# Second feed-forward products of a transformer block: residual rows loaded a tile a step, sums and stores of results spread over later steps, fewer buffers for the inputs of block two

## The chip, the cores and the metric

The kernel runs on one core of a Trainium2 chip. The metric is the device time of one execution in microseconds; the time of a kernel is the median of its runs. Beside the timed runs one execution was profiled. It has a time of its own, and all lines of the profile belong to that execution.

The engines in the profile: PE does matmuls (PEld loads their weights), DVE is the vector engine, ACT the scalar engine, POOL the third engine for elementwise work, and SP issues nearly all DMAs of this kernel. Each engine takes its instructions in the order of its own queue and waits at an instruction until what it needs is there.

## What is computed

One layer of a diffusion backbone over 2048 latent tokens of width 1024, with 256 context tokens: attention and a gated MLP side by side, their merge, and a feed-forward layer. All is float32. The change lies in the feed-forward layer:

```python
def sq_relu_mlp(h, w1, w2):
    return jnp.square(jax.nn.relu(h @ w1)) @ w2
...
        h2 = modulate(x, norm2_g[l], sh2, sc2)
        x = x + g2 * sq_relu_mlp(h2, w_ff1[l], w_ff2[l])
```

`x` is (2048, 1024), `w1` is (1024, 4096), `w2` is (4096, 1024). The residual `x`, which is added last, is the result of the merge; the kernel keeps it in DRAM (`x1_d`, shown as `x_d` in the profile).

## The kernel before

**Precision.** Each float32 operand is split into a high part (fp32r, the cast of L1291 on ACT) and a remainder (the subtraction of L1292 on DVE). A product is three matmuls: high by high, high by low, low by high (`product`, L1195 to L1197).

**Two blocks, seven products.** The tokens are worked in two blocks of 1024. In each block `ff1` makes the activations and `ff2` multiplies them by `w2`, both with Strassen's scheme in Winograd's form: the 2 x 2 grid of quarter matrices takes seven products of sums and differences instead of eight. `ff1` (L1256) writes its seven activation operands to DRAM (`ao_d`); the seven operands of `w2` are written once, in block one (`w2o_d` in the profile). `ff2` (L1296) reads both back.

**The steps of `ff2`.** The products come in the order 0, 1, 5, 6, 4, 2, 3. Each has 8 chunks (`NCH`) of its inner dimension, so there are 56 steps of one chunk. A step multiplies 4 tiles (`TT`) of 128 tokens by 512 columns, each in a PSUM bank of its own: 2 x 3 matmuls a tile. `ff2_chunk` (L1285) loads a chunk: for the activations and for the weights, one 512 KB load on SP, a cast on ACT, a subtraction on DVE. It is called two steps ahead; its four tiles have the tag f4, of which there are 12.

**What leaves.** After the last chunk of a product, `take` (L1327) empties the bank of each tile. Product 0 is copied to u2 (L1331) and stays in the bank; product 1 is added in the same bank and gives the first quarter of the result, whereupon u2 is copied back into the bank (L1334) and products 5 and 6 go on from there, each copied out as u2 and u3. Products 4 and 2 are added to u3 and u2 on DVE; product 3 goes on in the bank that product 6 left. A finished quarter goes through `leave` (L1318): a multiplication by the gate `g2b`, an addition of the residual tile `xs[t]`, and a store to `out`. All these additions and multiplications are recorded under L1304, the helper `tt`: f<-b,g2b is the multiplication from PSUM (products 1 and 3), f<-f,g2b that of products 4 and 2, f<-f,b the sum with u3 or u2, f<-f,f the residual's addition. `residual` (L1309) loads all four tiles of residual rows, 256 KB each, in the step of the last chunk. The stores (L1325) are put off by one step: they are issued after the chunk loads of the next step.

**The inputs of block two.** While `ff2` of block one runs, one piece of `h_ops` (L1004) is done after each step: in four passes of five pieces it fetches rows of `x1_d` (L985, four DMAs in pieces of 512 bytes, f8 tiles), scales them on DVE (L992), transposes them on PE (L182), reads the four transposed tiles out on ACT (L999), makes four sums and differences on DVE (L1019 to L1028) and splits seven tiles into halves (L970 on ACT, L971 on DVE).

**The f2 tiles.** u2, u3, xs, c, the transposed tiles of `h_ops` and its s1 to s4 all have the tag f2: 128 x 512 floats, 16 of them in all (L58).

**What sets the order.** The program names instructions in an order, but a planner puts each engine's queue together at build time by when it reckons operands to be ready. `order` (L1442) adds constraints to it: a tile of a tag begins after the tile of that tag named before it, and on SP the instructions named within `ff2` keep the program's order (`self.loads`). DVE's, ACT's and PE's order within `ff2` is the planner's.

Of the kernel before, what the change touches and what calls it, by code (L numbers as in the profile page):

```python
# [18 lines left out]
P = 128  # L19
# [10 lines left out]
TB = 512  # L30
NB = SEQ // TB
TT = TB // P
# [11 lines left out]
NCH = NG // 2  # L44
# [23 lines left out]
class Kern:  # L68
# [935 lines left out]
    def h_ops(self, blk, ops):  # L1004
        nc = self.nc
        add, sub = ALU.add, ALU.subtract
        at = self.here()
        rb = self.h_rstd(blk)
        self.pins.append(range(at, self.here()))
        for kk in range(KC // 2):  # L1010
            x = self.h_fetch(blk, kk)
            self.h_scaled(x, rb)
            yield
            raw = {(i, j): self.h_turn(x, kk, i, j) for j in range(2) for i in range(2)}
            yield
            s1, s2, s3, s4 = (self.sb("f2", [TB]) for _ in range(4))
            tt = nc.vector.tensor_tensor
            ops[0][kk] = self.halves(kk, 0, raw[0, 0])
            tt(out=s1, in0=raw[1, 0], in1=raw[1, 1], op=add)  # L1019
            tt(out=s2, in0=s1, in1=raw[0, 0], op=sub)  # L1020
            ops[5][kk] = self.halves(kk, 5, s2)
            yield
            ops[1][kk] = self.halves(kk, 1, raw[0, 1])
            tt(out=s3, in0=raw[0, 0], in1=raw[1, 0], op=sub)
            ops[6][kk] = self.halves(kk, 6, s3)
            yield
            ops[4][kk] = self.halves(kk, 4, s1)
            tt(out=s4, in0=raw[0, 1], in1=s2, op=sub)  # L1028
            ops[3][kk] = self.halves(kk, 3, raw[1, 1])
            ops[2][kk] = self.halves(kk, 2, s4)  # L1030
            yield

    def h_early(self):
# [262 lines left out]
    def ff2(self, blk, side):  # L1296
        nc = self.nc
        add, mult = ALU.add, ALU.mult
        ready = self.ready + [self.ff2_chunk(blk, 0, 1)]
        begin = self.here()  # L1300
        late = []

        def tt(out, in0, in1, op):
            nc.vector.tensor_tensor(out=out, in0=in0, in1=in1, op=op)  # L1304

        goes = {1: (0, 0), 4: (1, 1), 2: (0, 1), 3: (1, 0)}
        u2, u3, xs = ([None] * TT for _ in range(3))

        def residual(p):  # L1309
            i, j = goes[p]  # L1310
            for t in range(TT):
                xs[t] = self.sb("f2", [TB])
                nc.sync.dma_start(
                    xs[t],
                    self.x1_d[2 * blk + i][t * P : (t + 1) * P, j * TB : (j + 1) * TB],
                )

        def leave(p, t, src):  # L1318
            i, j = goes[p]
            row = (2 * blk + i) * TB + t * P  # L1320
            cs = slice(j * TB, (j + 1) * TB)
            c = self.sb("f2", [TB])
            tt(c, src, self.g2b[:, cs], mult)
            tt(c, c, xs[t], add)
            late.append(lambda: nc.sync.dma_start(self.out[0, row : row + P, cs], c))  # L1325

        def take(p, t):  # L1327
            ps = banks[p][t]
            if p == 0:
                u2[t] = self.sb("f2", [TB])  # L1330
                nc.scalar.copy(u2[t], ps)  # L1331
            elif p == 1:
                leave(p, t, ps)
                nc.scalar.copy(ps, u2[t])  # L1334
            elif p in (5, 6):
                u = u2 if p == 5 else u3
                u[t] = self.sb("f2", [TB])
                nc.scalar.copy(u[t], ps)
            elif p in (4, 2):
                u = u3[t] if p == 4 else u2[t]  # L1340
                tt(u, u, ps, add)
                leave(p, t, u)
            else:
                leave(p, t, ps)

        order = (0, 1, 5, 6, 4, 2, 3)
        steps = [(p, c) for p in order for c in range(NCH)]
        banks = {}
        for n, (p, c) in enumerate(steps):
            if n + 2 < len(steps):  # L1350
                ready.append(self.ff2_chunk(blk, *steps[n + 2]))
            for f in late:
                f()
            late.clear()
            (ah, al), (wh, wl) = ready.pop(0)
            fresh = p in (0, 4)
            if c == 0 and fresh:
                new = [self.bank([TB]) for _ in range(TT)]
                for other in (0, 1, 5, 6, 3) if p == 0 else (4, 2):
                    banks[other] = new  # L1360
            if c == NCH - 1 and p in goes:
                residual(p)
            for t in range(TT):
                tok = slice(t * P, (t + 1) * P)
                a = [(ah[:, s, tok], al[:, s, tok]) for s in range(2)]
                b = [(wh[:, s], wl[:, s]) for s in range(2)]
                self.product(banks[p][t], a, b, fresh and c == 0)
                if c == NCH - 1:
                    take(p, t)
            next(side, None)  # L1370
        for f in late:
            f()
        for _ in side:
            pass
        self.loads.append(range(begin, self.here()))
# [329 lines left out]
```

## Time and profile before

| what | us |
|---|---|
| median of 3 runs | 3104.24 |
| lowest and highest of them | 3098.3 and 3105.01 |
| the profiled execution | 3103.83 |
| its span, first to last instruction | 3102.0 |
| mean granted TensorE clock | 0.994 |

On the span's scale `ff2` of block one runs from about 2150 to 2475 us, `ff1` of block two from there to about 2780, and `ff2` of block two from there to the end at 3102. The timeline's rows give the start, the duration, the engine, the line, the operation, the tiles written and read, the shapes, a count where rows were merged, and in brackets the idle time of the engine before it with what ended it. SPq and DVEq are the queues' own instructions. A row of waits gives total us, number and longest. A row by windows gives, for each stretch, the busy time and count of PE, PEld, DVE, ACT and POOL, then the granted clock, the share of DMA and GB/s.

### The profile page before, as it was taken

Reading aid. Unit: us, or ns where it says so; the run is one execution under the profiler, and the core shown is the slowest. Engines: PE = TensorE matmul, PEld = TensorE weight load, DVE = VectorE, ACT = ScalarE, POOL = GpSimd, SP = SyncE. Lnnn points to the kernel's source line nnn. Section 1 sums busy time; section 2 is a strip of 40 time slices with the busy share of each in tenths; the row PEclk is TensorE's granted clock in tenths of the full one; section 3 lists DMA queues with packets and bytes.
Section 4 is the critical chain, followed back from the end, with each engine's and each line's share of the span. In section 5 each row is a group of like instructions: output and inputs, shape, how many; then the busy total and the mean of one; then the engine's idle time right before and its main releaser. Section 6 shows DMA issues by size and latency. Waiting matters only on the chain.

```text
span 3102.0 us, 37971 instructions
## 1 busy us (share of the span) xinstructions
PE 3042.7 (98%) x13892; PEld 2299.5 (74%) x13892; DVE 1972.1 (64%) x2893; ACT 1356.6 (44%) x2058; POOL 704.1 (23%) x539
## 2 busy tenths in 40 slices
PE   8999999999999999999999999999999999999999
PEld 4888888887555555555877878887777888888777
DVE  5837576576776767667643488876654676654545
ACT  4443435342555554544322255444543344444433
POOL 0000000010888888886144300000000000000000
PEclk9999999999999999999999999999999999999999
DMA  6354756544000000003754548887575644445565
GB/s 218 111 175 120 226 156 192 165 142 132 26 14 15 15 4 18 11 8 118 253 180 156 164 148 320 315 306 256 201 246 210 210 150 155 157 147 192 204 216 204
DMA packets 332173, 485.42 MB, mean 156 GB/s; under 512 B 33969, under 2 KB 166321, under 8 KB 331986
## 3 DMA queue, kind: packets, MB, share of 16 engines
q1 hardware_dynamic: 324002, 478.38, 46.3%
q10 hardware_dynamic: 7984, 4.61, 0.5%
q8 instruction: 109, 1.79, 0.2%
q14 instruction: 78, 0.64, 0.1%
HBM read 348.56 MB, written 134.35 MB: 156 GB/s over the span
## 4 chain that ended last, share of the span: by engine, by line
PE 89%; DMA 5%; DVE 3%; ACT 1%; issue 1%; POOL 1%; SPq 0%; DVEq 0%; ACTq 0%; POOLq 0%
PE b L1196 12%; PE b L1197 12%; PE b L1195 11%; PE b L176 10%; PE b L178 10%; PE b L177 10%; PE b L1597 8%; PE b L1564 5%; PE b L1583 4%; PE b L1529 3%; PE b L182 2%; DMA f<-w2o_d 1%; DMA bw<-in_w_br_gm 1%; POOL bw L148 1%; DMA f<-x_d 1%
## 5 line engine op out<-in xcount | busy, mean ns | idle before, releaser
L1292 DVE TENSOR_TENSOR f<-f,f 128x1024 fp32r<-128x1024 f32 x224 | 273.2, 1224 | 274.6 <-ACT f L1291 271.0
L1540 DVE TENSOR_REDUCE ts<-b 128x1 f32<-128x512 f32 x512 | 314.6, 681 | 173.2 <-PE b L1529 173.2
L1291 ACT CAST f<-f 128x1024 fp32r<-128x1024 f32 x224 | 235.2, 1053 | 335.3 <-DMA f<-ao_d 288.9
L1196 PE MATMUL b<-f,f 128*128 128x512 f32 x896 | 351.3, 392 | 4.6 <-DVE f L1292 4.0
L1197 PE MATMUL b<-f,f 128*128 128x512 f32 x896 | 349.6, 390 | 0.0
L1195 PE MATMUL b<-f,f 128*128 128x512 f32 x896 | 307.4, 392 | 10.3 <-ACT b L1334 4.7
L1613 POOL TENSOR_TENSOR ac<-ac,p 128x512 f32<-128x512 f32 x216 | 296.6, 1406 | 71.1 <-ACT p L1587 70.4
L1587 ACT ACTIVATE p<-b 128x512 f32<-128x512 f32 x384 | 199.4, 615 | 159.3 <-PE b L1583 142.5
L1613 POOL TENSOR_TENSOR ac<-ac,t 128x512 f32<-128x512 f32 x160 | 231.9, 1476 | 1.4 <-ACT t L1587 1.4
L1196 PE MATMUL b<-hl,f 128*128 128x512 f32 x576 | 224.9, 391 | 1.6 <-DVE hl L971 1.5
L1195 PE MATMUL b<-hl,f 128*128 128x512 f32 x576 | 224.1, 389 | 0.0
L1197 PE MATMUL b<-hl,f 128*128 128x512 f32 x576 | 224.0, 389 | 0.0
L148 DVE TENSOR_TENSOR w<-w,w 128x1024 fp32r<-128x1024 f32 x120 | 146.6, 1222 | 99.1 <-ACT w L144 70.6
L1195 PEld LDWEIGHTS b<-f,f 128*128 128x128 f32 x896 | 168.1, 188 | 51.0 <-ACT f L1291 6.8
L176 PE MATMUL b<-t,w 128*128 128x512 f32 x512 | 202.8, 396 | 0.1
L1196 PEld LDWEIGHTS b<-f,f 128*128 128x128 f32 x896 | 168.8, 188 | 45.7 <-DVE f L1292 11.2
L1564 PE MATMUL b<-t,t 128*128 128x512 f32 x576 | 198.4, 415 | 1.7 <-ACT p L1587 1.6
L178 PE MATMUL b<-t,w 128*128 128x512 f32 x512 | 199.7, 390 | 0.0
L177 PE MATMUL b<-t,w 128*128 128x512 f32 x512 | 199.5, 390 | 0.0
L1197 PEld LDWEIGHTS b<-f,f 128*128 128x128 f32 x896 | 168.5, 188 | 34.6
L176 PE MATMUL b<-w,t 128*128 128x512 f32 (+1 forms) x528 | 191.0, 362 | 1.0 <-ACT t L440 1.0
L144 ACT CAST w<-w 128x1024 fp32r<-128x1024 f32 x120 | 126.1, 1050 | 150.0 <-DMA w<-in_w_in 118.3
(226 smaller groups left out, 6289.6 us busy)
## 6 DMA issues: line engine op xcount, KB each, us to landing
w<-in_w_in SPq DMA_DIRECT2D x120, 512.0 KB
ao_d<-f SPq DMA_DIRECT2D x224, 256.0 KB
f<-ao_d SPq DMA_DIRECT2D x112, 512.0 KB
f<-w2o_d SPq DMA_DIRECT2D x112, 512.0 KB
f<-in_w_ff SPq DMA_DIRECT2D x48, 1024.0 KB
w2o_d<-f SPq DMA_DIRECT2D x112, 256.0 KB
md<-in_w_mod SPq DMA_DIRECT2D x32, 512.0 KB
f<-x_d SPq DMA_DIRECT2D x64, 256.0 KB
```

The source lines that it names most:

```text
L176: mm(ps, sh, mh, start=start, stop=False)
L177: mm(ps, sh, ml, start=False, stop=False)
L178: mm(ps, sl, mh, start=False, stop=stop)
L1195: mm(ps, wh, hh, start=start and k == 0, stop=False, skip_group_check=True)
L1196: mm(ps, wh, hl, start=False, stop=False, skip_group_check=True)
L1197: mm(ps, wl, hh, start=False, stop=k == len(w) - 1, skip_group_check=True)
L1291: nc.scalar.copy(h, f32(l))
L1292: nc.vector.tensor_tensor(out=l, in0=f32(l), in1=f32(h), op=ALU.subtract)
L1540: nc.vector.tensor_reduce(out=self.mx[:, t, h, c : c + 1], in_=ps[h], axis=AX.X, op=ALU.max)
L1564: self.nc.tensor.matmul(self.pts[j][h], k.KA[c][self.kv][:, ks], self.qa[h], start=True, stop=False, skip_group_check=True,)
L1597: nc.tensor.matmul(self.o[h * HD : (h + 1) * HD, :], k.V[c][:, i, self.kv * HD : (self.kv + 1) * HD], pt[h], start=j == 0, stop=j == NKT - 1,)
L1613: nc.gpsimd.tensor_tensor(out=self.acc[e][:, h], in0=old[:, h], in1=pt[h], op=ALU.add)
```

## The change

In `h_ops`, the differences are written over transposed tiles that are no longer needed, so that a pass takes five f2 tiles instead of eight; the difference for product 6 is made one piece earlier. In `ff2`, `residual` loads one tile, and is called in each of the last four steps of a product that leaves, with the tile's number. `leave` only multiplies; the addition of the residual and the store are put on the list `late` together. From that list one entry is taken before tile 0 and one before tile 2 of a step, except in a product's last step, so that the four entries go in two steps. After the last product they are all worked off behind the loop, as the stores were before.

```diff
--- before.py
+++ after.py
@@ -1013,21 +1013,22 @@
             yield
             raw = {(i, j): self.h_turn(x, kk, i, j) for j in range(2) for i in range(2)}
             yield
-            s1, s2, s3, s4 = (self.sb("f2", [TB]) for _ in range(4))
             tt = nc.vector.tensor_tensor
-            ops[0][kk] = self.halves(kk, 0, raw[0, 0])
-            tt(out=s1, in0=raw[1, 0], in1=raw[1, 1], op=add)
-            tt(out=s2, in0=s1, in1=raw[0, 0], op=sub)
-            ops[5][kk] = self.halves(kk, 5, s2)
+            r00, r01, r10, r11 = (raw[i, j] for i in range(2) for j in range(2))
+            s1 = self.sb("f2", [TB])
+            ops[0][kk] = self.halves(kk, 0, r00)
+            tt(out=s1, in0=r10, in1=r11, op=add)
+            tt(out=r10, in0=r00, in1=r10, op=sub)
+            tt(out=r00, in0=s1, in1=r00, op=sub)
+            ops[5][kk] = self.halves(kk, 5, r00)
             yield
-            ops[1][kk] = self.halves(kk, 1, raw[0, 1])
-            tt(out=s3, in0=raw[0, 0], in1=raw[1, 0], op=sub)
-            ops[6][kk] = self.halves(kk, 6, s3)
+            ops[1][kk] = self.halves(kk, 1, r01)
+            tt(out=r00, in0=r01, in1=r00, op=sub)
+            ops[6][kk] = self.halves(kk, 6, r10)
             yield
             ops[4][kk] = self.halves(kk, 4, s1)
-            tt(out=s4, in0=raw[0, 1], in1=s2, op=sub)
-            ops[3][kk] = self.halves(kk, 3, raw[1, 1])
-            ops[2][kk] = self.halves(kk, 2, s4)
+            ops[3][kk] = self.halves(kk, 3, r11)
+            ops[2][kk] = self.halves(kk, 2, r00)
             yield
 
     def h_early(self):
@@ -1306,23 +1307,25 @@
         goes = {1: (0, 0), 4: (1, 1), 2: (0, 1), 3: (1, 0)}
         u2, u3, xs = ([None] * TT for _ in range(3))
 
-        def residual(p):
+        def residual(p, t):
             i, j = goes[p]
-            for t in range(TT):
-                xs[t] = self.sb("f2", [TB])
-                nc.sync.dma_start(
-                    xs[t],
-                    self.x1_d[2 * blk + i][t * P : (t + 1) * P, j * TB : (j + 1) * TB],
-                )
+            xs[t] = self.sb("f2", [TB])
+            nc.sync.dma_start(
+                xs[t], self.x1_d[2 * blk + i][t * P : (t + 1) * P, j * TB : (j + 1) * TB]
+            )
 
         def leave(p, t, src):
             i, j = goes[p]
             row = (2 * blk + i) * TB + t * P
             cs = slice(j * TB, (j + 1) * TB)
-            c = self.sb("f2", [TB])
+            c, x = self.sb("f2", [TB]), xs[t]
             tt(c, src, self.g2b[:, cs], mult)
-            tt(c, c, xs[t], add)
-            late.append(lambda: nc.sync.dma_start(self.out[0, row : row + P, cs], c))
+
+            def rest():
+                tt(c, c, x, add)
+                nc.sync.dma_start(self.out[0, row : row + P, cs], c)
+
+            late.append(rest)
 
         def take(p, t):
             ps = banks[p][t]
@@ -1349,18 +1352,17 @@
         for n, (p, c) in enumerate(steps):
             if n + 2 < len(steps):
                 ready.append(self.ff2_chunk(blk, *steps[n + 2]))
-            for f in late:
-                f()
-            late.clear()
             (ah, al), (wh, wl) = ready.pop(0)
             fresh = p in (0, 4)
             if c == 0 and fresh:
                 new = [self.bank([TB]) for _ in range(TT)]
                 for other in (0, 1, 5, 6, 3) if p == 0 else (4, 2):
                     banks[other] = new
-            if c == NCH - 1 and p in goes:
-                residual(p)
+            if c >= NCH - TT and p in goes:
+                residual(p, c - (NCH - TT))
             for t in range(TT):
+                if late and t % 2 == 0 and c < NCH - 1:
+                    late.pop(0)()
                 tok = slice(t * P, (t + 1) * P)
                 a = [(ah[:, s, tok], al[:, s, tok]) for s in range(2)]
                 b = [(wh[:, s], wl[:, s]) for s in range(2)]
```

## The prediction

> **What bounds the kernel now.** I read the page first, then the table by stage, then the waits of PE inside the two second products, and last the timelines of the engines around the longest of those waits.
>
> ```profile
> span 3102.0 us, 37971 instructions
> PE 3042.7 (98%) x13892; PEld 2299.5 (74%) x13892; DVE 1972.1 (64%) x2893; ACT 1356.6 (44%) x2058; POOL 704.1 (23%) x539
> ```
>
> ```profile
> 2140.00:2460.00 320.00, 307.37 (x1351) 249.25 (x1350) 188.51 (x207) 146.57 (x172) 0.00 (x0) 0.99 0.65 222
> 2460.00:2780.00 320.00, 320.00 (x1412) 264.55 (x1411) 211.71 (x267) 148.46 (x212) 0.00 (x0) 1.00 0.42 148
> 2770.00:3097.00 327.00, 321.23 (x1400) 261.29 (x1398) 159.92 (x154) 127.46 (x133) 0.00 (x0) 1.00 0.59 205
> ```
>
> PE is busy for 98% of the span, so the matmuls set the time, and the change touches no matmul. What it can move is idle time of PE in the two runs of `ff2`: 12.6 us of the first row (320 less 307.4; block one) and 5.8 us of the third (block two). The row between, `ff1` of block two, has no idle time at all, and DVE's 212 us there do not hurt. The same row gives the pace: 1412 matmuls in 320 us, 0.227 us each. A step of `ff2` has 4 tiles of 2 x 3 matmuls, so 24 x 0.227 = 5.44 us; a tile takes 1.36 us.
>
> Who ends PE's idle time, block one first, then block two:
>
> ```profile
> PE b L1195 <- ACT b L1334: 2.4, 2, 1.7
> PE b L1196 <- DVE f L1292: 2.4, 3, 1.0
> PE b L1195 <- ACT f L1291: 2.1, 4, 0.7
> PE b L182 <- DVE f L992: 1.9, 1, 1.9
> PE b L1195 <- ACT f L1331: 1.8, 1, 1.8
> PE b L182 <- PE b L1197: 1.0, 1, 1.0
> ```
>
> ```profile
> PE b L1195 <- ACT b L1334: 2.2, 2, 1.6
> PE b L1196 <- DVE f L1292: 1.6, 2, 1.0
> PE b L1195 <- ACT f L1291: 1.5, 3, 0.5
> ```
>
> The columns are total us, times, longest. L1334, first in both, is the copy that puts u2 back into the bank when product 1 has been taken out; it waits for `leave`, whose lines the change edits. In block two the three L1291 waits stand at the ends of products 0, 5 and 6, where nothing leaves and the change edits nothing; L1331 is the copy at the end of product 0.
>
> The end of product 1 in block two, on PE, DVE and ACT:
>
> ```profile
> 2870.37 0.39 PE L1197 MATMUL b<-f,f 128*128 128x512 f32 x1
> 2872.34 0.50 PE L1195 MATMUL b<-f,f 128*128 128x512 f32 x1 [1.57 <-ACT b L1334]
> 2872.67 0.39 PE L1196 MATMUL b<-f,f 128*128 128x512 f32 x1
> 2873.60 0.40 PE L1197 MATMUL b<-f,f 128*128 128x512 f32 x1
> 2874.67 0.50 PE L1195 MATMUL b<-f,f 128*128 128x512 f32 x1 [0.67 <-ACT b L1334]
> ```
>
> ```profile
> 2869.83 1.23 DVE L1292 TENSOR_TENSOR f<-f,f 128x1024 fp32r<-128x1024 f32 x1 [2.65 <-ACT f L1291]
> 2870.98 0.68 DVE L1304 TENSOR_TENSOR f<-b,g2b 128x512 f32<-128x512 f32 x1
> 2871.58 1.22 DVE L1292 TENSOR_TENSOR f<-f,f 128x1024 fp32r<-128x1024 f32 x1
> 2872.71 0.68 DVE L1304 TENSOR_TENSOR f<-f,f 128x512 f32<-128x512 f32 x1
> 2873.31 1.28 DVE L1304 TENSOR_TENSOR f<-b,g2b 128x512 f32<-128x512 f32 x2
> ```
>
> ```profile
> 2871.69 0.59 ACT L1334 COPY b<-f 128x512 f32<-128x512 f32 x1 [0.49 <-DVE f L1304]
> 2874.03 1.19 ACT L1334 COPY b<-f 128x512 f32<-128x512 f32 x2 [1.74 <-DVE f L1304]
> ```
>
> PE ended this product at about 2870.8, so its tile 0 three tiles (4.1 us) earlier, long before 2870.98. But its multiplication (f<-b,g2b) stands in DVE's queue behind the remainder of a chunk that is needed a step later (2869.83, which waited 2.65 us for its cast). Then come the chunk's second remainder, the first addition (2872.71) and only then the multiplication of tile 1. PE loses a start at 2872.34 and another at 2874.67.
>
> What a stall costs beyond the idle time shown: from 2870.37 to 2872.34 are 1.97 us instead of 0.23, and the matmul after it comes after 0.33 instead of 0.23. That is 1.84 us for 1.57 us idle, so I add 0.27 per stall.
>
> **The change part by part.** The sum is made against the profiled execution, 3103.83 us (span 3102.0 and 1.83 around it); the median of the runs is 3104.24, 0.41 above it.
>
> *A. End of product 1.* Block two pays 2.2 + 2 x 0.27 = 2.78 us, block one 2.4 + 2 x 0.27 = 2.94, together 5.72. The change takes the four additions out of `leave`, and three of the four residual loads out of the last step. The additions alone: tile 1's multiplication comes 0.60 us earlier (2872.71 to 2873.31), which takes 0.60 off the second stall, 1.2 us over the blocks. The larger part hangs on the order in which the planner puts DVE's work. `c` is an f2 tile, and `order` makes every f2 tile begin after the f2 tiles named before it, so tile 0's multiplication cannot be planned ahead of all four residual loads of that step; with one a step, three are past by then. I expect the multiplication in front of the remainders, as the sums of products 4 and 2 stand already. Those ends then still pay for a remainder pushed behind: 1.0 + 0.27 = 1.27 us (the longest L1196 wait in block two). So 5.72 - 2 x 1.27 = 3.2 us gained. Bounds: nothing (an addition that is ready takes the same slot as before) and 5.7.
>
> *B. Stores after products 4 and 2.* In block two, after product 2:
>
> ```profile
> 3056.94 5.08 SPq L1325 DMA_DIRECT2D out_x<-f  x4
> 3062.11 0.39 SPq L1290 DMA_DIRECT2D f<-ao_d  x1
> ```
>
> ```profile
> 3069.12 1.19 PE L1195 MATMUL b<-f,f 128*128 128x512 f32 x4
> 3070.38 0.50 PE L1196 MATMUL b<-f,f 128*128 128x512 f32 x1
> ```
>
> The four stores hold SP's queue for 5.1 us, each waiting for its addition, and the next chunk's load gets behind them. PE shows it at 3070.38: three matmuls after 3069.12 would put it at 3070.03, so 0.35 late, and with 0.11 after it 0.46 us. With two stores a step the queue is free after the second. There are four such ends; this is the largest one, so the gain lies between 0.5 and 1.8; I take the middle, 1.1.
>
> *C. SP's pile-up in block one*, where the inputs of block two are fetched at the same time:
>
> ```profile
> 2211.24 2.13 SPq L985 DMA_DIRECT2D f<-x_d  x4
> 2242.94 1.83 SPq L1313 DMA_DIRECT2D f<-x_d  x4
> 2244.82 4.89 SPq L985 DMA_DIRECT2D f<-x_d  x4
> 2259.74 1.99 SPq L1290 DMA_DIRECT2D f<-w2o_d  x1
> ```
>
> ```profile
> 2254.41 2.29 DVE L992 TENSOR_TENSOR f<-f,fs 128x2048 f32<-128x2048 f32 x1 [0.54 <-DMA f<-x_d]
> ```
>
> The fetch (L985) takes 2.13 us to issue when it is alone and 4.89 us right behind four residual loads. Its scaling starts at 2254.41, after the four additions and a wait for the fetch, and PE's transposes wait 1.0 us for it (L182 in block one). With three loads moved to earlier steps the fetch is some 2.7 us earlier and the additions no longer stand before it: 1.0 + 0.27 = 1.3 us gained, or nothing. The pile also delays the load at 2259.74 and with it one of the four L1291 waits (2.1 / 4 + 0.27 = 0.8); I count it as gone, with nothing as its other end.
>
> *D. Fewer f2 tiles in `h_ops`.* The same four sums and differences, the same seven halves; one difference is made a step earlier, three f2 tiles less per pass. No wait of PE quoted above ends on an f2 tile coming free, so I take 0. It may let the planner place the transposed tiles better: the L1331 wait and the other L1291 waits of block one are then in reach, 1.8 + 0.27 and about 2 x 0.8. The first has a sequel:
>
> ```profile
> 2195.00:2200.00 5.00, 3.16 (x12) 2.25 (x11) 3.12 (x4) 5.00 (x9) 0.00 (x0) 0.89 0.62 202
> 2200.00:2205.00 5.00, 5.00 (x19) 3.99 (x18) 4.94 (x7) 5.00 (x10) 0.00 (x0) 0.77 0.02 8
> ```
>
> After 1.8 us idle the granted clock fell to 0.89 and 0.77 for five us each, (0.11 + 0.23) x 5 = 1.7 us lost. So D lies between 0 and 5.4 us gained; a poorer placing could cost about as much as one such wait, 2 us.
> The Trainium skill (TensorE: Matmul & The Clock Gate, Part 1) says that the clock is halved after an idle window of about 3.4 us. By that rule no stall here would cost clock, and the upper end of D would be 3.7; the row shows a loss after 1.8 us, and I go by the row.
>
> *E. What is added.* Two additions per step in two steps after each leaving product, 2 x 0.68 us on DVE beside two remainders of 1.22, 3.8 of 5.44 us: covered. Two stores per step on SP ahead of the next step's loads: covered as long as their additions are done when the next loads fall due; without that cover, see the second rival. At the very end the additions come after the loop:
>
> ```profile
> 3096.27 1.43 DVE L1304 TENSOR_TENSOR f<-b,g2b 128x512 f32<-128x512 f32 x2
> 3097.61 1.28 DVE L1304 TENSOR_TENSOR f<-f,f 128x512 f32<-128x512 f32 x2
> ```
>
> Two of the four additions already run behind the last multiplication. The planner may keep the other two between, since tiles 0 and 1 are ready earlier (0), or move them behind (2 x 0.60 = 1.2 us). I take 0.
>
> Sum: 3.2 + 1.1 + 1.3 + 0.8 = 6.4 us; 3103.83 - 6.4 = 3097.4.
>
> **The rivals.**
>
> *1. The queue order stays.* The multiplication of tile 0 stays behind the remainders, because additions that are ready early fill the same slots. For it: the planner goes by when operands are ready, as the tail shows, where additions and multiplications are mixed. Against it: the loads that held `c` back are gone from that step. Then A gives between 0 and 1.2, B 0.5, C 1.3 at best: 2 us, about 3101.8.
>
> *2. Stores block the loads; slower.* SP's order is fixed in `ff2`, so a store that waits for its addition stops the next step's two loads. Should DVE put the additions behind the remainders of the chunk whose load was issued in that same step, the store comes late in each of the two steps after products 1, 4 and 2, 12 steps in all.
>
> ```profile
> 2865.13 0.36 SPq L1290 DMA_DIRECT2D f<-ao_d  x1
> ```
>
> This chunk is usable at 2871.58 + 1.22 = 2872.8, 7.7 us after its issue, and two steps are 10.9 us: the loads may be late by 3.2 us. From there on every step pays. If each pays as much as the late load above, 0.8 us, that is 10 us, and with B lost and A and C cut to 2.5, 3103.83 + 10 - 2.5 = 3111. Against it: four stores held the queue for 5.1 us before, and PE lost 0.46.
>
> *3. Block one gains as well.* D's upper end on top of the forecast: 3097.4 - 5.4 = 3092.0. For it: ACT's and DVE's queues are fullest there. Against it: no wait is shown to end on an f2 tile.
>
> **How the numbers follow.** Forecast 0.47, rival 1 0.29, rival 2 0.12, rival 3 0.12. About 0.2% (6.2 us) is what a measurement of this kernel can tell from no change: faster means under 3098.0, slower over 3110.4, from the median. The forecast lies on that line, since A alone can move by 3; I give 0.28 of its 0.47 to faster. Rival 3 is faster, 0.12; of rival 1 0.04 is (if C and B come in whole). Faster 0.44, slower 0.12, same 0.44. The range runs from 3090 (rival 3 with A at a better value) to 3106 (rival 1 with E's 1.2 and the 2 us of D as costs, 3105.0, and a bit of the spread of the median); rival 2 is left out.
>
> **What would show it.** In the profile after: waits of L1195 on L1334 falling from 2 to at most 1 per block and below 1.3 us; the f<-b,g2b multiplications of product 1 starting within 1 us of their PE tile; stores in pairs, with the loads of the next chunk a regular 5.44 us apart; L985's last fetch issued in about 2.1 us and no L182 wait near it. The sum is wrong if L1334 still ends two waits per block (rival 1), if L1290 waits for L1325's additions and L1291 or L1292 waits grow in the steps after products 1, 4 and 2 (rival 2), or if the L1331 wait and the clock drop vanish (rival 3).

## The result, and the profile after

The changed kernel takes 3097.14 us (median of 20 runs, 3090.99 to 3101.66) against 3101.97 us before (20 runs, 3097.21 to 3108.91): 4.8 us less. The ratio is 0.9983, with a 95% interval of 0.9976 to 0.9989, so 3.4 to 7.4 us. The time lies 0.3 us from the forecast, but that closeness is luck. The gain is 1.6 us smaller than the 6.4 us of the sum, and the kernel before came out 1.9 us lower over 20 runs than the profiled execution from which the sum was taken; the two errors cancel. The ratios here and below compare fast runs alone, which leaves out one execution of 10062 us in the last experiment but one.

The page of the profile after, first lines; its profiled execution took 3101.04 us:

```profile
span 3099.3 us, 37971 instructions
PE 3039.4 (98%) x13892; PEld 2298.5 (74%) x13892; DVE 1973.4 (64%) x2893; ACT 1354.7 (44%) x2058; POOL 703.5 (23%) x539
```

The spans differ by 2.7 us only, but the two executions differ before `ff2` as well: its first product starts at 2144.8 us in the trace before and at 2149.1 after, in a part of the program that is the same. So I count inside `ff2`. A number that serves for every run below: over the matmuls of one block's `ff2`, by how much the distances between starts exceed 0.227 us, distances less than 0.06 over left out. I call it PE's loss. Before, it is 19.1 us in block one and 9.4 in block two; after, 15.0 and 7.7. That is 5.8 us less, of which 1.8 is clock (matmuls up to 0.43 us apart instead of 0.23, after two falls of the granted clock; last section). The number does not see slow transposes, whose starts stay under 0.227 us apart.

PE's waits after, in block one and then in block two (total us, times, longest):

```profile
PE b L1197 <- DVE f L1293: 3.3, 5, 1.0
PE b L1196 <- ACT f L1334: 1.8, 1, 1.8
PE b L182 <- DVE f L992: 1.8, 1, 1.8
PE b L1196 <- ACT f L1292: 1.7, 3, 0.7
PE b L1196 <- ACT b L1337: 0.6, 1, 0.6
PE b L182 <- PE b L1198: 0.5, 1, 0.5
```

```profile
PE b L1197 <- DVE f L1293: 1.7, 2, 1.0
PE b L1196 <- ACT b L1337: 1.5, 1, 1.5
PE b L1196 <- ACT f L1292: 1.5, 3, 0.5
```

L1337 is the former L1334, the copy of u2 into the bank: one wait a block in place of two. The others stand much as they were: L1334 (formerly L1331) with 1.8, L1292 (formerly L1291) with 1.7 after 2.1 in block one and 1.5 in block two, L1293 (formerly L1292) even up in block one.

The end of product 1 in block two, DVE and the matmul that waits:

```profile
2868.77 1.23 DVE L1293 TENSOR_TENSOR f<-f,f 128x1024 fp32r<-128x1024 f32 x1 [2.49 <-ACT f L1292]
2869.91 2.48 DVE L1305 TENSOR_TENSOR f<-b,g2b 128x512 f32<-128x512 f32 x4
2872.30 1.21 DVE L1293 TENSOR_TENSOR f<-f,f 128x1024 fp32r<-128x1024 f32 x1
2873.44 2.49 DVE L1305 TENSOR_TENSOR f<-f,f 128x512 f32<-128x512 f32 x4
```

```profile
2871.27 0.50 PE L1196 MATMUL b<-f,f 128*128 128x512 f32 x1 [1.51 <-ACT b L1337]
```

The four multiplications now stand together, ahead of the second remainder and of all additions: the second stall is gone. But the first remainder, which waited 2.49 us for its cast, still stands before them, and the first stall is nearly what it was (1.51 against 1.57).

SP's queue after product 2 of block two, and in block one where the inputs of block two are fetched:

```profile
3056.52 0.95 SPq L1326 DMA_DIRECT2D out_x<-f  x2
3057.57 0.41 SPq L1291 DMA_DIRECT2D f<-ao_d  x1
3058.63 0.89 SPq L1326 DMA_DIRECT2D out_x<-f  x2
```

```profile
2243.29 0.46 SPq L1313 DMA_DIRECT2D f<-x_d  x1
2243.80 2.39 SPq L985 DMA_DIRECT2D f<-x_d  x4
2258.36 1.56 SPq L1291 DMA_DIRECT2D f<-w2o_d  x1
```

Two stores take 0.95 us where four took 5.08, and the chunk's load follows at 3057.57 instead of 3062.11. The first matmul of product 3 that waits starts at 3051.27 after and at 3053.49 before, so the load is 2.3 us earlier in the step's own time. The fetch issues in 2.39 us instead of 4.89. The load that came at 2259.74 is still late, at 2258.36: in both traces it stands 10.4 to 10.5 us ahead of the first matmul that waits for its chunk.

And the end of product 0 in block one, where the clock fell before (0.89 and 0.77 in these two stretches):

```profile
2195.00:2200.00 5.00, 3.42 (x24) 2.73 (x22) 0.92 (x1) 4.00 (x6) 0.00 (x0) 1.00 0.16 59
2200.00:2205.00 5.00, 4.75 (x21) 3.92 (x22) 3.92 (x6) 4.07 (x7) 0.00 (x0) 1.00 0.49 184
```

The wait for L1334 is as long, 1.8 us, and the granted clock stays at 1.00.

### The profile page after: what moved, and what is told of

The parts are those of the page before. It is cut to its first block, busy times and chain, and to the rows that moved or that the text cites. A ratio compares the mean times of both kernels' runs of the same rounds, so it can differ in the third digit from the quotient of the medians.

```text
span 3099.3 us, 37971 instructions
## 1 busy us (share of the span) xinstructions
PE 3039.4 (98%) x13892; PEld 2298.5 (74%) x13892; DVE 1973.4 (64%) x2893; ACT 1354.7 (44%) x2058; POOL 703.5 (23%) x539
## 4 chain that ended last, share of the span: by engine, by line
PE 88%; DMA 4%; DVE 4%; ACT 2%; POOL 1%; issue 1%; SPq 0%; DVEq 0%; ACTq 0%; POOLq 0%
PE b L1197 12%; PE b L1198 12%; PE b L1196 12%; PE b L176 10%; PE b L178 10%; PE b L177 10%; PE b L1599 8%; PE b L1566 5%; PE b L1585 4%; PE b L1531 3%; PE b L182 2%; DMA bw<-in_w_br_gm 2%; POOL bw L148 1%; DVE f L1293 1%; DMA ts<-in_b_mod 1%
## 5 line engine op out<-in xcount | busy, mean ns | idle before, releaser
L1293 DVE TENSOR_TENSOR f<-f,f 128x1024 fp32r<-128x1024 f32 x224 | 272.3, 1223 | 262.8 <-ACT f L1292 259.6
L1292 ACT CAST f<-f 128x1024 fp32r<-128x1024 f32 x224 | 234.5, 1052 | 322.9 <-DMA f<-ao_d 283.2
```

The lines of the kernel that those rows point to most:

```text
L1292: nc.scalar.copy(h, f32(l))
L1293: nc.vector.tensor_tensor(out=l, in0=f32(l), in1=f32(h), op=ALU.subtract)
```

## The experiments

The theory going in: the gain comes from the order of DVE's queue at the end of product 1 and from SP's queue behind the stores, both in `ff2`. The rival: the smaller number of f2 tiles carries it, in block one.

**The parts apart.** Four kernels, each a part of the change on top of the kernel before.

*The changed `ff2`, the old `h_ops`.*

> The changed second products (loads a tile a step, additions and stores spread) with the eight f2 tiles per pass of before. My theory, that the gain is the order of DVE's queue at the end of product 1 and SP's queue behind the stores: about 4.5 us faster than before, nearly all of the change's 5 us, and the L1334 or L1337 wait of block one falls to one. The rival, that fewer f2 tiles carry it: within 1.5 us of before.

Ratio to before 0.9989 (0.9979 to 0.9998), 3.4 us. PE's loss in block two is 7.8 us, close to the changed kernel's 7.7. In block one it is 18.4, but 2.8 of that is clock: the granted clock fell twice (0.50 in the stretch 2160 to 2165, 0.66 in 2250 to 2255). Without the clock it is 15.6, against 17.3 before and 15.0 in the changed kernel. The L1336 wait (the u2 copy) is one, as expected, but a long one:

```profile
PE b L1195 <- ACT b L1336: 2.8, 1, 2.8
PE b L182 <- DVE f L992: 2.8, 1, 2.8
```

*The changed `h_ops` alone.*

> Only the five f2 tiles per pass in the inputs of block two; second products as before. My theory: within 1 us of before, the two stalls at the end of product 1 (1.7 and 0.8 us) stay in both blocks, and the clock drop after the end of product 0 in block one may come or not. The rival, that the buffers carry the gain: 3 to 5 us faster, with the waits of block one shorter.

Ratio 1.0009 (0.9999 to 1.0018): no gain. The clock did not drop in `ff2`, and PE's loss is 20.9 and 10.0 us, so block one loses 3.6 us more than the kernel before without its clock. The rival gets nothing from this run.

*The loads alone:* `residual(p, t)` in each of the last four steps, `leave` as before.

> Only the residual rows a tile a step; additions and stores as before. My theory: the fetch L985 issues in 2.1 us in place of 4.9 and the multiplications of product 1 come before the additions in DVE's queue, so 1 to 2.5 us faster; the stores still hold SP for 5 us and the late loads after products 4 and 2 stay. The rival, that spreading the additions and stores alone matters: no difference.

Ratio 0.9996 (0.9987 to 1.0005), undecided between the two. In block two PE loses 8.5 us instead of 9.4, and most of the difference lies where stores and loads met. So the late loads did not stay, against the expectation: the four stores after product 2 still hold SP for 4.48 us (5.08 before), but the losses three steps on are gone. The multiplications do not all come before the additions either; two of each alternate. In block one the fetch issues in 2.39 us and no transpose waits for it, but the end of product 1 costs 6.0 us, with one wait of 2.9:

```profile
PE b L1195 <- ACT b L1332: 2.9, 1, 2.9
```

Of these 6.0 us, 3.0 are clock, which fell about the end of this wait:

```profile
2245.00:2250.00 5.00, 3.44 (x8) 2.80 (x9) 5.00 (x9) 2.60 (x4) 0.00 (x0) 0.58 1.09 381
2250.00:2255.00 5.00, 5.00 (x18) 3.90 (x18) 4.56 (x5) 1.61 (x3) 0.00 (x0) 0.73 0.89 340
```

Block one loses 17.3 us in all, 14.4 without the clock.

*The sums and stores alone:* `leave` and `late` as in the change, `residual` in the last step.

> Only the additions and stores spread; four residual loads in the last step as before. My theory: the second stall of product 1 goes (0.6 to 0.9 us a block) and the late loads after products 4 and 2 go (1.1 us), so 2 to 3 us faster; L985 still takes 4.9 us to issue. The rival, that the loads in one step are what keeps the multiplications back: under 1.2 us, only the stores' part.

Ratio 1.0005 (0.9995 to 1.0015): the expected 2 to 3 us did not come. Block two falls to 8.0 us, by more than the loads bring. Block one loses 20.0 us, 18.3 without the clock (0.73 in the stretch 2265 to 2270); there other waits grow:

```profile
PE b L1195 <- ACT f L1291: 3.6, 4, 1.9
```

So in block two each half of the `ff2` edit helps: the end of product 1 costs 2.80 us before, 2.57 with the loads alone, 2.11 with the sums alone, 1.86 with both. In block one it is the loads that carry the gain. I add up, without the clock, what PE loses at the end of product 1, at the transposes one step on and at the late load three steps on. That is 5.3 us before, 6.6 with `h_ops` alone and 6.4 with the sums alone, all with four residual loads in one step. With one load a step it is 3.5 with the loads alone, 3.5 with the changed `ff2`, and 2.9 in the changed kernel.

*Are the buffers it?* The changed kernel, its sums named in the new order but written to tiles of their own:

```diff
-            tt(out=r10, in0=r00, in1=r10, op=sub)
-            tt(out=r00, in0=s1, in1=r00, op=sub)
-            ops[5][kk] = self.halves(kk, 5, r00)
+            s2, s3, s4 = (self.sb("f2", [TB]) for _ in range(3))
+            tt(out=s3, in0=r00, in1=r10, op=sub)
+            tt(out=s2, in0=s1, in1=r00, op=sub)
+            ops[5][kk] = self.halves(kk, 5, s2)
...
```

> The changed kernel with the sums of h_ops in its new order, but written to tiles of their own: eight f2 tiles a pass again. If the three tiles are what the second products of block one lack, PE loses at the end of product 1 of block one about 4.5 us (as with the changed second products alone) in place of 1.8, and the kernel is 2 to 3 us slower than the changed one. If the earlier difference was what mattered, it stays at the changed kernel's 1.8.

Ratio to before 0.9979 (0.9971 to 0.9988); PE's loss is 13.8 and 7.7 us. Eight tiles do as well as five. The expectation that they would cost 2 to 3 us fell: the three tiles bring nothing that these runs can see. (The 1.8 us of the expectation belong to block two; in block one the end of product 1 costs 1.0 in the changed kernel and 1.9 here, and the waits behind it are shorter by nearly as much.) The new order of the sums brings little under the changed `ff2`: the old `h_ops` lost 3.4 us more in block one than the changed kernel, but 2.8 of that is the clock.

*The changed kernel again.*

> The changed kernel once more, on the same chip as these. Both theories: 4 to 6 us under before. If the drop of the clock after the end of product 0 in block one belongs to the kernel before alone, it stays away here; if it comes by chance, it may be here too.

Ratio 0.9988 (0.9979 to 0.9997), 3.7 us; PE's loss 15.2 and 7.8. The same kernel has the same stalls, and the clock did not drop in `ff2`.

**What is left, and why.** The stalls that the change leaves stand at the ends of products. First I took the order out of the planner's hands, in block two alone: a chunk's cast and remainder are named a step after its load, and ACT and DVE keep the program's order.

```diff
+            held = blk == 1
             if n + 2 < len(steps):
-                ready.append(self.ff2_chunk(blk, *steps[n + 2]))
+                load = self.ff2_load if held else self.ff2_chunk
+                ready.append(load(blk, *steps[n + 2]))
+            if held and n and n + 1 < len(steps):
+                self.ff2_convert(ready[1])
...
+            held = held or (idx in rows and i.engine in both)
```

> The changed kernel; in block two a chunk's cast and remainder are named a step after its load, ACT's and DVE's queues keep the program's order, and the last product's additions follow their multiplications. If the queue order is what costs at the ends of products, the 7.7 us that PE loses in block two fall below 2.5 us, and the time is 5 to 7 us under the changed kernel's. If the loads or the PSUM copies themselves were late, the stalls stay within 2 us of before and so does the time.

3071.97 us, ratio to before 0.9903 (0.9889 to 0.9916). In block two PE's loss is 0.0. All waits of PE over both blocks that the profile names:

```profile
PE b L183 <- issue: 1.2, 1, 1.2
```

That is far more than the 5 to 7 us expected, because block one fell from 15.0 to 1.8 us too, and nothing was fixed there. Doing the same in block one (PE's order fixed as well, pieces of `h_ops` after the second tile, their rows fetched two steps ahead):

> As the order experiment in block two, and in block one too: there PE's order is the program's as well, a piece of h_ops stands after a step's second tile, and its rows are fetched two steps ahead. If the queue order is the cause in both blocks, PE loses under 5 us in block one in place of 15 and under 2.5 us in block two; 13 to 17 us under the changed kernel. If block one is held up by the work itself (DVE's and ACT's share, loads), only block two's 5 to 7 us.

3075.2 us, ratio 0.9913 (0.9899 to 0.9927), PE's loss 3.2 and 0.0 us. It repairs block one no better than the kernel that left its order alone. So something that both share did it. `ff2_chunk` had been split in two, and with that it names both loads of a chunk ahead of the two casts, in block one as well. That edit by itself, on the changed kernel:

```diff
         for src in (self.ao_d[blk][p][c], self.wo_d[p][c]):
             l, h = self.sb("f4", [2, TB], F32R), self.sb("f4", [2, TB], F32R)
             nc.sync.dma_start(f32(l), src.rearrange("s p c -> p s c"))
+            out.append((h, l))
+        for h, l in out:
             nc.scalar.copy(h, f32(l))
             nc.vector.tensor_tensor(out=l, in0=f32(l), in1=f32(h), op=ALU.subtract)
-            out.append((h, l))
```

> The changed kernel with one edit: a chunk names both loads before its two casts and remainders. Theory: the planner must begin the f4 tiles in the order in which they are first written, so the second load is planned only after the first chunk half's cast, the planner believes the chunks late, and puts their remainders behind the work at a product's end; with both loads first, the stalls at the ends of products 0, 5, 6, 4 and 2 go (about 6 us a block) and the time is 15 us or more under the changed kernel's. If it was the fixed order of the earlier experiments that helped, this edit gives no more than 3 us.

3075.63 us, ratio to before 0.9903 (0.9887 to 0.9919). PE's loss is 0.6 and 0.0 us, and the profile names no wait of PE in `ff2` any more. The stretch of block one, by windows, and DVE at the end of product 1 of block two:

```profile
2148.00:2468.00 320.00, 319.95 (x1445) 265.63 (x1444) 206.55 (x228) 153.27 (x178) 0.00 (x0) 1.00 0.68 230
```

```profile
2848.81 0.68 DVE L1306 TENSOR_TENSOR f<-b,g2b 128x512 f32<-128x512 f32 x1
2849.82 0.69 DVE L1306 TENSOR_TENSOR f<-b,g2b 128x512 f32<-128x512 f32 x1 [0.33 <-PE b L1198]
2851.45 1.23 DVE L1295 TENSOR_TENSOR f<-f,f 128x1024 fp32r<-128x1024 f32 x1 [0.93 <-ACT f L1294]
```

```profile
2846.87 0.36 SPq L1291 DMA_DIRECT2D f<-ao_d  x1
2852.31 0.36 SPq L1291 DMA_DIRECT2D f<-ao_d  x1
```

Two multiplications stand before the remainder that used to hold them (the first two of the four need only their tiles), and the second waits for PE itself. The loads on SP come 5.44 us apart, 2846.87 and 2852.31, the pace of the steps, and the changed kernel's load at 2869.57 follows one at 2864.13 by the same 5.44. The first remainder starts 4.58 us after its load here (2851.45) and 4.64 us in the changed kernel (2868.77):

```profile
2864.13 0.36 SPq L1291 DMA_DIRECT2D f<-ao_d  x1
2869.57 0.36 SPq L1291 DMA_DIRECT2D f<-ao_d  x1
```

The data did not come earlier. Only the order of the queues is another. ACT shows it at the end of product 0 of block two, in the changed kernel and then with both loads first:

```profile
2817.97 1.05 ACT L1292 CAST f<-f 128x1024 fp32r<-128x1024 f32 x1 [1.92 <-DMA f<-ao_d]
2821.74 0.59 ACT L1334 COPY f<-b 128x512 f32<-128x512 f32 x1 [2.72 <-PE b L1198]
2824.49 1.05 ACT L1292 CAST f<-f 128x1024 fp32r<-128x1024 f32 x1
```

```profile
2801.59 1.05 ACT L1294 CAST f<-f 128x1024 fp32r<-128x1024 f32 x1 [1.47 <-DMA f<-ao_d]
2802.79 1.05 ACT L1294 CAST f<-f 128x1024 fp32r<-128x1024 f32 x1
2804.94 0.59 ACT L1335 COPY f<-b 128x512 f32<-128x512 f32 x1 [1.10 <-PE b L1198]
```

A chunk's second cast stands behind three copies to u2 that wait for PE, 6.5 us after the first one; with both loads first it comes 1.2 us after it, ahead of all copies. So the order of the queues is the cause of the stalls at the ends of products, shown by this pair of kernels. Why the planner chose the old order is argued from the code, and no run lifts the constraint by itself: `order` lets a tile of a tag begin only after the one whose first write was named before it, so the second load (an f4 tile) is planned after the first half's cast (another), one after the other, though in the changed kernel's trace SP issues the two 0.45 us apart (2864.13 and 2864.58). A planner that reckons chunks late puts their remainders behind the work of a product's end.

The same edit on the kernel before:

> The kernel before with the same edit of the chunk. Theory: the ends of products 0, 5, 6, 4 and 2 are repaired here too, and the end of product 1 keeps its multiplication behind remainders, as the change is missing: 10 to 17 us under before, and 2 to 6 us over the changed kernel with the edit. If the change and the edit repair the same stalls, both kernels come out the same within 1.5 us.

Ratio to before 0.9924 (0.991 to 0.9938), about 24 us, more than the 10 to 17 expected. PE's loss is 2.8 and 2.5 us; what stays is mostly the end of product 1, in both blocks:

```profile
PE b L1195 <- ACT b L1335: 3.0, 2, 1.5
PE b L1196 <- DVE f L1294: 0.4, 1, 0.4
```

With the edit, the change still takes away 4.7 us of PE's loss (5.3 to 0.6), and the two repairs add up. The ratios, 0.9903 and 0.9924, agree with that, but their intervals overlap. Last, the conversions named a step later in both blocks with no order fixed:

> The changed kernel with a chunk's conversions named a step after its loads in both blocks, and no order fixed. Theory: as for loads first, 15 us or more under the changed kernel, with block two free of stalls; the fixed order adds nothing. If the fixed order is needed, stalls of over 1 us remain at the ends of products.

3077.56 us, ratio 0.9906 (0.9891 to 0.9921), PE's loss 0.8 and 0.0 us. The fixed order is not needed, and naming the conversions later adds nothing to naming both loads first. The simple edit is enough to beat both kernels.

## Why the prediction was right, and where it was not

The time and the direction are right, and so is the place: PE's loss fell in `ff2`, mostly at the end of product 1 and behind the stores. Term by term, from the two traces:

- **A, end of product 1 (3.2 us).** It brought 0.94 us in block two (2.80 to 1.86) and about 2.0 in block one (3.00 to 0.98), 3.0 in all. The size is right, the picture is not. I expected the multiplications in front of both remainders, and what is left to be a remainder pushed behind them. They came between the remainders; the first remainder still stands ahead, and what is left is the wait for the u2 copy, 1.5 us in block two where I had put it below 1.3. The reason I gave, that the f2 tile `c` cannot be planned ahead of four residual loads, is not the one that holds the first multiplication: one residual load a step leaves it there, and both loads of a chunk named first takes it away.
- **B, stores (1.1 us).** The four late places cost 0.19, 0.29, 0.29 and 0.45 us before and nothing after: 1.2 us, by the queue that the prediction named. Pairs of stores are not needed for it, though: the loss is gone as well with the loads alone, where four stores go out together.
- **C, the pile-up (1.3 + 0.8 us).** The fetch issues as fast as forecast, 2.39 us. But the transposes still wait 0.5 us (0.76 us of loss instead of 1.25), since DVE scales at 2253.55, after three of the additions that I took to be gone, and the late load stayed late (2258.36): that place costs 1.17 us instead of 1.05. So 0.4 us in place of 2.1. This is the mis-sized term. The sum took it to be independent of A, and in block one it is not. With the changed `ff2` alone and with the loads alone, C came nearly whole (from 2.3 to 0.5 us) and A not at all (3.0 us, clock left out). In the five profiles with one load a step and the old order of loads and casts, the two together leave 2.9 to 3.5 us. That the fetch and the late load catch up while PE stands at the end of product 1 fits this, but no run shows it by itself.

```profile
2251.74 1.89 DVE L1305 TENSOR_TENSOR f<-f,f 128x512 f32<-128x512 f32 x3
2253.55 2.28 DVE L992 TENSOR_TENSOR f<-f,fs 128x2048 f32<-128x2048 f32 x1
```

- **D, fewer f2 tiles (0).** Right: eight tiles do as well as five. Its upper end held a clock loss of 1.7 us that did vanish in the profile after, yet not by the change: the wait before it is as long as it was.
- **E, the tail (0).** Right: additions and multiplications are mixed at the end as before, and 5.43 us pass from the last matmul's start to the end of the span in both traces.

A + B + C come to 4.6 us. In block one a new wait of 0.8 us in product 1 (at 2212.87) stands against them, so that 4.0 us of PE's loss are gone without the clock. The measured 4.8 us (3.4 to 7.4) fits that. How often the clock fell in the timed runs is not known, so a part of it may still be clock. The forecast's 6.4 was 1.8 too much against the terms, nearly all of it in C.

Of the rivals, the first was half right: tile 0's multiplication did stay behind a remainder, but the additions did not take the early slots. The second did not show: the waits of the steps after products 4 and 2 are gone, and the one after product 1 grew by 0.1 us only. The third would have needed L1331's wait to vanish, and it stayed. Of the signs that I had named, one wait a block on the u2 copy and stores in pairs came. Two did not: the multiplications of product 1 in block two start about 4 us after their first tile is done, not within 1 us, and the loads around the stores are 8.4 us apart (3049.16 and 3057.57), not 5.44. What I did not see at all is that the waits that I set aside as untouched by the change (L1291, L1331, L1292 at the ends of all products) had one cause, more than five times the size of what the change repairs (22.1 us of PE's loss against 4.0, clock left out).

## What to carry to other kernels

Where a planner orders the queues, look at which instruction stands before the late one, and ask why the planner thought that order good. A constraint that means only order (here: tiles of a tag begin in the order of their first writes) can make it plan two transfers one after the other that in the trace are issued 0.45 us apart; naming both loads before the work on either took 22 us of PE's loss out, and the change's own edits 4. And measure the parts of a change in each stage apart, with the loss of clock taken out: the spread sums gained 1.4 us in block two and lost 1.0 in block one, where the planner had other work to place, and the gain of the loads in block one was hidden by a fall of the clock.

## What the runs showed of the hardware

The clock drop after the end of product 0 in block one came by chance. The wait there is 1.8 us long in eight profiles (before, after, the changed kernel again, the four parts and the fresh tiles); in one of them the granted clock fell to 0.89 and 0.77, in seven it stayed at 1.00 in the 20 us around.

It was not the only drop. The profile before has another one, behind the first wait of the transposes in block one, which 1.9 us of idle time precede:

```profile
2155.00:2160.00 5.00, 3.12 (x15) 2.62 (x14) 3.52 (x2) 2.22 (x3) 0.00 (x0) 0.80 0.99 345
2160.00:2165.00 5.00, 5.00 (x23) 4.33 (x23) 2.79 (x4) 4.24 (x6) 0.00 (x0) 0.86 0.06 22
```

The 16 transposes there take 3.52 us, and 1.97 in the profile after, where the clock stayed. Over the `ff2` stretches of the eight profiles, PE has 13 waits of 1.8 to 2.1 us, and the clock fell at 3 of them; it fell at all 3 waits of 2.8 to 2.9 us (two with the changed `ff2` alone, one with the loads alone) and at no shorter wait. So a longer wait seems to make the drop likelier, but 16 waits are few.

The Trainium skill (TensorE: Matmul & The Clock Gate, Part 1) says that the clock is decided over free-running windows of about 3.4 us, so that its changes vary from run to run. The chance character agrees with that; a loss after only 1.8 us idle is shorter than the idle window that the page gives. One drop is worth up to 1.7 us of PE's loss (1.6 after the end of product 0), a third of what the change brings: two profiles alone would have credited it to the change, and three of the four parts would be misjudged in block one with it left in.
